# Joining token-major weight units to 512 columns and queueing weight splits behind the activations' low parts

## The chip, the cores and the metric

The kernel runs on one core of one Trainium2 chip. The metric is the device time of one execution in microseconds (us). Before the change it is 937.9 us, the median of three runs (937.23 to 940.86 us).

## The reference

The program is a chain of five residual stages on 256 tokens of width 1024, all in fp32:

```
h = swiglu(rms(x), ffn1_w_in, ffn1_w_out)          # 1024 -> 2 x 2816 -> 1024
x = x + 0.5 * rms(h)
x = x + rms(token_mixing(rms(x)))                  # retention + neighbourhood attention
h = swiglu(rms(x), ffn2_w_in, ffn2_w_out)
x = x + 0.5 * rms(h)
x = x + recurrent_mixer(rms(x))                    # y * silu(gate), width 1536
x = x + shortconv_mixer(rms(x))                    # bg * conv(cg * xv) * silu(gate), width 1536
return rms(x)
```

with `swiglu(x) = (silu(g) * u) @ w_out`, where g and u are the two halves of `x @ w_in`. Each stage begins with a normalised x and a product with a wide in-projection, and ends with an out-projection back to 1024 columns that is added to x. Nothing of the next stage's first product can start before x of a token is complete and its mean square is known.

## The kernel before

**Precision.** Every fp32 product is made of three faster ones. An operand is split into a high part (a rounded copy) and a low part (what the rounding left); `mm3` (L231 to L233) multiplies high by high, then the two mixed products. For weights the copy is L88 on ACT and the subtraction L90 on DVE, each over a part of 128 x 1024 numbers. For activations they are called ph and pl; those of the normed tile are L370 (ACT) and L371 (DVE).

**Weights.** All weights are listed in the order of use, in units of 256 columns cut into parts of 512 KB. `Stream` loads raw parts (L75, SP's queue), splits them (L88, L90) and hands them out from a ring of 41 slots. At most four raw parts wait unsplit, and up to 15 parts (AHEAD) are split ahead of the one in use; `use(p, most)` splits up to `most` parts on top of what p needs.

**Token tiles.** The 256 tokens are two tiles of 128, t = 0 and t = 1. `phase_b` is the out-projection. Its last parts are multiplied first for t = 0 and then for t = 1, so that `add_block` (L351, L354, L357) and the norm (`norm_of_x`, `inv_rms`) of t = 0 run beside the matmuls of t = 1. Four entries before the end, `ready(0)` has TensorE transpose the normed tile hn of t = 0 (L366, eight times 128 x 128), and ph and pl are taken out of PSUM. `phase_a` is the next in-projection. Its first `late` units are computed token-major: the activation is the stationary operand, 128 tokens by 256 weight columns, first for t = 0 and, after `ready(1)`, for t = 1. The result is then turned by transposes (`turn_tok`). All later units have the weights stationary and all 256 tokens of two column blocks as one 512-wide result. In the mixing stage the units computed first (queries and keys) are token-major anyway, with 512 columns.

**Order.** The tile framework's scheduler places every engine's instructions by its own model of time. `S.hold` names two instructions; splits that are issued later are kept behind them on ACT and on DVE. In the kernel before only the norm of x sets it. The bias loads of the attention (L118) and the mask additions on them (L624) are also placed by the scheduler, at the beginning of the mixing stage.

Of the kernel before, what the change touches and what calls it, by code (L numbers as in the profile page):

```python
# [29 lines left out]
class Part:  # L30


    def __init__(self, ap, whole):
        self.ap, self.whole = ap, whole
        self.a, self.n = ap.shape[1], ap.shape[1] * ap.shape[2]
        self.raw = self.hi = self.lo = None
# [5 lines left out]
class Unit:  # L42
    def __init__(self, ap, whole=False, most=1024):
        self.a = ap.shape[1]
        h = max(1, self.a * ap.shape[2] // most)
        h = self.a // h
        self.parts = [Part(ap[:, k:k + h, :], whole) for k in range(0, self.a, h)]


class Stream:  # L50
# [19 lines left out]
    def load(self, most=100):  # L70
        while (most and self.nd < len(self.parts) and self.nd - self.ns < self.ahead
# [3 lines left out]
            self.loaded = self.nc.sync.dma_start(out=p.raw, in_=p.ap)  # L75
# [50 lines left out]
def block_kernel(ctx: ExitStack, tc: tile.TileContext, A, C, out):  # L126
# [26 lines left out]

    def b_units(w):
# [31 lines left out]
    u_f2 = ffn_units(A["ffn2_w_in"], A["ffn2_w_out"])  # L186
# [173 lines left out]
    def transpose_pair(src, t, pair, k0, n):  # L360

        for b in range(0, n, 4):
# [7 lines left out]
            act.activation(out=h, in_=pv, func=AF.Copy)  # L370
            dve.tensor_tensor(out=lo, in0=pv, in1=h.bitcast(F32), op=ALU.subtract)  # L371
# [809 lines left out]
```

## Time and profile before

| | before |
|---|---|
| median of three runs | 937.9 us |
| profiled execution | 936.56 us |
| span, first to last instruction | 934.8 us |
| mean granted clock of TensorE | 0.997 of full speed |
| PE, DVE, ACT busy | 98%, 60%, 50% of the span |
| DMA, mean | 180 GB/s |

Mixing, the second feed-forward stage, recurrent and shortconv begin, by the transposes of their normed tile of t = 0, at 199, 438, 630 and 749 us. The profiled execution is 1.34 us shorter than the median of the runs, and 1.76 us of it lie outside the span. TensorE's matmuls overlap in the records (a 256-column one is shown as 0.28 us long but the next begins 0.12 us later), so their pace is read from start to start, not from their durations.

### The profile page before, as it was taken

What the parts mean: (1) busy time and instruction counts of PE and PEld (TensorE: products, weight loads), DVE (VectorE), ACT (ScalarE), POOL (GpSimd) and SP (SyncE); (2) the same over time, 40 slices, a digit from 0 to 9 for tenths busy, and PEclk for the clock granted to TensorE, in tenths of its full rate; (3) what the DMA queues carried; (4) which work ended last, traced back from release to release, by engine and by line L of the source; (5) the groups of instructions that cost most, each with busy time, mean ns of one, the idle gap of its engine ahead of it and who ended that gap; (6) DMA issues with size and microseconds to landing.
All of it is one profiled execution on the core that took longest, in us unless ns stands there. A gap on an engine that the chain in (4) does not pass through costs nothing.

```text
span 934.8 us, 15539 instructions
## 1 busy us (share of the span) xinstructions
PE 914.8 (98%) x6378; PEld 853.9 (91%) x6378; DVE 561.7 (60%) x736; ACT 471.9 (50%) x666; POOL 13.1 (1%) x24
## 2 busy tenths in 40 slices
PE   8999999999999999999999999999999989999997
PEld 7999998877978899997999998888998889999986
DVE  7854647377745454667574445545787965756513
ACT  7744546245565444545554444434769845544401
POOL 0000000000000000000000000000000000000000
PEclk9999999999999999999999999999999999999999
DMA  9955557758436453676455556757426745645501
GB/s 317 339 182 158 175 169 248 258 108 253 150 106 217 133 161 114 225 236 208 142 181 165 165 158 211 242 165 246 137 91 211 235 151 183 221 165 186 160 1 46
DMA packets 132333, 168.70 MB, mean 180 GB/s; under 512 B 12065, under 2 KB 112165, under 8 KB 132262
## 3 DMA queue, kind: packets, MB, share of 16 engines
q1 hardware_dynamic: 131828, 167.11, 56.1%
q8 instruction: 50, 0.82, 0.4%
q10 hardware_dynamic: 434, 0.59, 0.2%
q14 instruction: 21, 0.17, 0.1%
HBM read 166.64 MB, written 1.05 MB: 179 GB/s over the span
## 4 chain that ended last, share of the span: by engine, by line
PE 86%; DVE 5%; ACT 4%; issue 2%; SPq 1%; DMA 1%; POOL 0%; POOLq 0%; DVEq 0%; ACTq 0%
PE bank L233 27%; PE bank L231 27%; PE bank L232 27%; DVE lo L90 2%; SPq L118 1%; DVE ri L1030 1%; PE bank L743 1%; PE bank L768 1%; DMA t<-in_na_rel_bias 1%; ACT hi L88 1%; PE bank L366 1%; ACT ri L971 1%; ACT u L970 0%; PE bank L456 0%; PE bank L653 0%
## 5 line engine op out<-in xcount | busy, mean ns | idle before, releaser
L90 DVE TENSOR_TENSOR lo<-raw,hi 128x1024 fp32r<-128x1024 f32 (+1 forms) x302 | 359.1, 1216 | 130.3 <-ACT hi L88 75.1
L231 PE MATMUL bank<-ph,hi 128*128 128x256 f32 x1360 | 387.0, 285 | 0.0
L232 PE MATMUL bank<-pl,hi 128*128 128x256 f32 x1360 | 384.9, 283 | 0.0
L233 PE MATMUL bank<-ph,lo 128*128 128x256 f32 x1360 | 384.8, 283 | 0.0
L88 ACT ACTIVATE hi<-raw 128x1024 fp32r<-128x1024 f32 (+1 forms) x302 | 306.3, 1048 | 148.5 <-PE bank L233 70.3
L232 PEld LDWEIGHTS bank<-pl,hi 128*128 128x128 f32 x1360 | 261.0, 192 | 0.2
L231 PEld LDWEIGHTS bank<-ph,hi 128*128 128x128 f32 x1360 | 261.0, 192 | 0.2
L233 PEld LDWEIGHTS bank<-ph,lo 128*128 128x128 f32 x1360 | 261.0, 192 | 0.0
L231 PE MATMUL bank<-hi,ph 128*128 128x512 f32 (+1 forms) x636 | 225.6, 356 | 4.2 <-ACT ph L370 4.1
L233 PE MATMUL bank<-hi,pl 128*128 128x512 f32 (+1 forms) x636 | 222.4, 354 | 5.4 <-DVE pl L371 5.4
L232 PE MATMUL bank<-lo,ph 128*128 128x512 f32 (+1 forms) x636 | 223.3, 353 | 0.0
L231 PEld LDWEIGHTS bank<-hi,ph 128*128 128x128 f32 x636 | 121.2, 191 | 23.6 <-ACT ph L370 6.8
L233 PEld LDWEIGHTS bank<-hi,pl 128*128 128x128 f32 x636 | 120.3, 190 | 22.8 <-DVE pl L371 6.9
L232 PEld LDWEIGHTS bank<-lo,ph 128*128 128x128 f32 x636 | 121.2, 191 | 15.6
L470 ACT ACTIVATE ph<-tmp 128x512 fp32r<-128x512 f32 x28 | 17.6, 629 | 58.4 <-DVE tmp L492 53.8
L321 ACT ACTIVATE tmp<-x 128x512 f32<-128x512 f32 (+1 forms) x25 | 15.4, 614 | 50.1 <-DVE x L346 34.0
L492 DVE TENSOR_TENSOR tmp<-tmp,bank 128x512 f32<-128x512 f32 x19 | 13.0, 686 | 33.8 <-PE bank L233 33.8
L471 DVE TENSOR_TENSOR pl<-tmp,ph 128x512 fp32r<-128x512 f32 x28 | 19.2, 691 | 13.0 <-ACT ph L470 13.0
L354 DVE TENSOR_TENSOR tmp<-bank,g 128x512 f32<-128x512 f32 x12 | 8.3, 689 | 29.9 <-ACT tmp L351 29.9
L351 ACT ACTIVATE tmp<-bank 128x512 f32<-128x512 f32 x12 | 7.2, 600 | 36.3 <-PE bank L233 36.1
L371 DVE TENSOR_TENSOR pl<-bank,ph 128x512 fp32r<-128x512 f32 x24 | 15.7, 686 | 12.9 <-ACT ph L370 12.9
L313 POOL TENSOR_TENSOR small<-small,half 128x1 f32<-128x1 f32 x18 | 10.8, 601 | 811.1 <-DVE small L311 811.1
(141 smaller groups left out, 434.1 us busy)
## 6 DMA issues: line engine op xcount, KB each, us to landing
raw<-in_ffn_w_in SPq DMA_DIRECT2D x86, 512.0 KB, 4.6
raw<-in_w_mix_in SPq DMA_DIRECT2D x52, 512.0 KB, 4.5
raw<-in_b_w_in SPq DMA_DIRECT2D x48, 512.0 KB, 4.5
raw<-in_ffn_w_out SPq DMA_DIRECT2D x44, 512.0 KB, 4.1
raw<-in_a_w_in SPq DMA_DIRECT2D x24, 512.0 KB, 4.0
raw<-in_a_w_out SPq DMA_DIRECT2D x12, 512.0 KB, 3.6
raw<-in_b_w_out SPq DMA_DIRECT2D x12, 512.0 KB, 3.9
raw<-in_w_ret_out SPq DMA_DIRECT2D x8, 512.0 KB, 4.5
```

The costliest lines, as they stand in the source:

```text
L88: self.copied = self.nc.scalar.activation(out=p.hi, in_=p.raw, func=AF.Copy)
L90: self.nc.vector.tensor_tensor(out=p.lo, in0=p.raw, in1=p.hi.bitcast(F32), op=ALU.subtract)
L118: self.nc.sync.dma_start(out=out, in_=ap)
L231: pe.matmul(ps, a[0], b[0], start=first, stop=False)
L232: pe.matmul(ps, a[0], b[1], start=False, stop=False)
L233: pe.matmul(ps, a[1], b[0], start=False, stop=last)
L313: nc.gpsimd.tensor_tensor(out=r, in0=v, in1=half[:, 0:1], op=ALU.pow)
L321: sq = act.activation(out=tmp()[:, :c1 - c0], in_=x[:, t, c0:c1], func=AF.Square, scale=1.0 / 32, accum_out=ss[:, c:c + 1])
L371: dve.tensor_tensor(out=lo, in0=pv, in1=h.bitcast(F32), op=ALU.subtract)
L470: act.activation(out=h, in_=src, func=AF.Copy)
L471: dve.tensor_tensor(out=lo, in0=src, in1=h.bitcast(F32), op=ALU.subtract)
L492: dve.tensor_tensor(out=sg, in0=sg, in1=b, op=ALU.mult)
```

## The change

1. Two 256-column units that are used token-major become one unit of 512 columns (`pair_unit`): gate and up columns in the two feed-forward stages (one such pair in the first, in parts of half the size, two in the second), two gate units in the recurrent stage (one 256-column unit stays beside them), and the four column groups of the first block in shortconv, as two pairs. A part of a pair is two row blocks by 2 x 256 columns and is loaded by two DMAs of 256 KB. The products that follow the matmul (`tok_evac`) are now made in token-major form, before the turn; shortconv so turns two results where it turned four.
2. `ready(0)` is called six entries before the end of `phase_b` instead of four, and until then the t = 1 entries ask for no split ahead. In `phase_a` the t = 0 pass asks for none either before `ready(1)`, which comes `lead` parts before the end of that pass (0 in the first feed-forward stage, 2 in the second, 1 in recurrent, 2 in shortconv; in mixing 2 parts before).
3. `ready()` sets `S.hold` to its own two last evictions, so that weight splits issued later stand behind ph on ACT and pl on DVE.

```
             p.raw = p.view(self.slot(F32, "raw"))
-            self.loaded = self.nc.sync.dma_start(out=p.raw, in_=p.ap)
+            if len(p.ap.shape) == 3:
+                self.loaded = self.nc.sync.dma_start(out=p.raw, in_=p.ap)
+            else:
+                to = p.raw.rearrange("p a (z c) -> p a z c", z=p.ap.shape[2])
+                for z in range(p.ap.shape[2]):
+                    self.loaded = self.nc.sync.dma_start(out=to[:, :, z, :], in_=p.ap[:, :, z, :])
             self.nd += 1
             most -= 1
...
+    def pair_unit(w, c0, c1, most=1024):
+
+        v = w[:, c0:c0 + 256].rearrange("(k p) c -> p k c", p=128)
+        l = [list(d) for d in v.ap]
+        return Unit(bass.AP(tensor=v.tensor, offset=v.offset, ap=[l[0], l[1], [c1 - c0, 2], l[2]]), most=most)
+
...
-    def ffn_units(win, wout, small=False):
-        g, u = a_units(win, 0, DFF), a_units(win, DFF, 2 * DFF)
-        if small:
-            g[0] = Unit(win[:, 0:256].rearrange("(k p) c -> p k c", p=128), most=512)
-        return add([x for p in zip(g, u) for x in p]), add(b_units(wout))
-
-    u_f1 = ffn_units(A["ffn1_w_in"], A["ffn1_w_out"], True)
+    def ffn_units(win, wout, tok, most=1024):
+        first = [pair_unit(win, c, DFF + c, most) for c in range(0, 256 * tok, 256)]
+        g, u = a_units(win, 256 * tok, DFF), a_units(win, DFF + 256 * tok, 2 * DFF)
+        return add(first), add([x for p in zip(g, u) for x in p]), add(b_units(wout))
+
...
-    u_ag = a_units(A["a_w_in_2"], 0, WIDTH)
-    add(u_ag[:EARLY] + [ax[0], ax[1], u_gw[0], ax[2], u_gw[1], ax[3], ax[4], u_gw[2], ax[5]] + u_ag[EARLY:])
+    u_ag = a_units(A["a_w_in_2"], 256 * EARLY, WIDTH)
+    u_at = [pair_unit(A["a_w_in_2"], 0, 256)] + a_units(A["a_w_in_2"], 512, 256 * EARLY)
+    add(u_at + [ax[0], ax[1], u_gw[0], ax[2], u_gw[1], ax[3], ax[4], u_gw[2], ax[5]] + u_ag)
...
-    u_b = [[Unit(bw[:, s * WIDTH + c:s * WIDTH + c + 256].rearrange("(k p) c -> p k c", p=128))
-            for s in (1, 2, 0, 3)] for c in range(0, WIDTH, 256)]
-    for us in u_b:
-        add(us)
+    u_bt = add([pair_unit(bw, WIDTH, 2 * WIDTH), pair_unit(bw, 0, 3 * WIDTH)])
+    u_b = add([Unit(bw[:, s * WIDTH + c:s * WIDTH + c + 256].rearrange("(k p) c -> p k c", p=128))
+               for c in range(256, WIDTH, 256) for s in (1, 2, 0, 3)])
...
-    def mm_tok(bk, u, xt, t):
-
-        for q, p in enumerate(u.parts):
-            if t == 0:
-                S.use(p, 1)
-            for j in range(p.a):
-                k = q * p.a + j
-                mm3(bk[:, t * 256:(t + 1) * 256], xt.at(k, t * 128, t * 128 + 128),
-                    (p.hi[:, j, :], p.lo[:, j, :]), k == 0, k == u.a - 1)
-            if t == 1:
-                S.done(p)
+    def mm_tok(ps, u, q, xt, t):
+
+        p = u.parts[q]
+        for j in range(p.a):
+            k = q * p.a + j
+            mm3(ps, xt.at(k, t * 128, t * 128 + 128), (p.hi[:, j, :], p.lo[:, j, :]), k == 0, k == u.a - 1)
 
     def mm_t(ps, p, xt, t, k0, nk):
...
-            act.activation(out=h, in_=pv, func=AF.Copy)
-            dve.tensor_tensor(out=lo, in0=pv, in1=h.bitcast(F32), op=ALU.subtract)
+            a = act.activation(out=h, in_=pv, func=AF.Copy)
+            d = dve.tensor_tensor(out=lo, in0=pv, in1=h.bitcast(F32), op=ALU.subtract)
+        return a.ins, d.ins
...
-            transpose_pair(self.hn[t], t, self.pair, 0, NKD)
+            S.hold = transpose_pair(self.hn[t], t, self.pair, 0, NKD)
...
-            if q == len(order) - 4 and not last:
+            if q == len(order) - 6 and not last:
                 nxt.ready(0)
                 S.reserve = 0
             if a[0] is acc[t][0]:
-                S.use(p, 1)
+                S.use(p, 1 if t == 0 or last or nxt.pair else 0)
             mm_b(a, p, xt, t, k, n)
             if a[-1] is acc[t][-1]:
...
-    def phase_a(us, nxt, evac, late, tok_evac=None):
+    def phase_a(tok, us, nxt, evac, tok_evac, lead):
+
 
 
         xt = nxt.pair
         banks = []
-        for u in us[:late]:
-            b = bank()
-            banks.append(b)
-            mm_tok(b, u, xt, 0)
-        nxt.ready(1)
-        turned = None
-        for i, u in enumerate(us):
-            if i < late:
-                b = banks[i]
-                mm_tok(b, u, xt, 1)
+        for u in tok:
+            if u.w == 512:
+                banks.append([bank(), bank()])
             else:
                 b = bank()
-                mm_a2(b, u, xt)
+                banks.append([b[:, 0:256], b[:, 256:512]])
+        n = sum(len(u.parts) for u in tok)
+        for u, b in zip(tok, banks):
+            for q, p in enumerate(u.parts):
+                if n == lead:
+                    nxt.ready(1)
+                S.use(p, 0 if n > lead else 1)
+                mm_tok(b[0], u, q, xt, 0)
+                n -= 1
+        if lead == 0:
+            nxt.ready(1)
+        turned = None
+        for i, (u, b) in enumerate(zip(tok, banks)):
+            for q, p in enumerate(u.parts):
+                S.use(p, 1)
+                mm_tok(b[1], u, q, xt, 1)
+                S.done(p)
+            if turned:
+                turned()
+            turned = tok_evac(i, b)
+        for i, u in enumerate(us):
+            b = bank()
+            mm_a2(b, u, xt)
             if turned:
                 turned()
                 turned = None
-            if i < late:
-                turned = (tok_evac or turn_evac(evac))(i, b)
-            else:
-                evac(i, b)
+            evac(i, b)
         return xt
...
         for t in range(2):
-            if t == 1:
-                nxt.ready(1)
             for z in range(2):
                 ps = [p for u in qk_units[z] for p in u.parts]
                 for i, p in enumerate(ps):
-                    if t == 0:
-                        S.use(p)
+                    if (t, z, i) == (0, 1, 2):
+                        nxt.ready(1)
+                    S.use(p, 1 if (t, z, i) >= (0, 1, 2) else 0)
                     mm_t(acc[z][t], p, xt, t, 2 * i, NKD)
                     if t == 1:
                         S.done(p)
...
         def tok_evac(i, b):
-            if i % 2 == 0:
-                held[i] = b
-                return None
-            g = held.pop(i - 1)
             sg = tmp()
-            act.activation(out=sg, in_=g, func=AF.Silu)
-            dve.tensor_tensor(out=sg, in0=sg, in1=b, op=ALU.mult)
-            return lambda: split_pair(f, i - 1, 2, two(turn_tok(sg)))
-
-        xt = phase_a(us[0], nxt, evac, late, tok_evac)
+            for t in range(2):
+                s = sg[:, t * 256:(t + 1) * 256]
+                act.activation(out=s, in_=b[t][:, 0:256], func=AF.Silu)
+                dve.tensor_tensor(out=s, in0=s, in1=b[t][:, 256:512], op=ALU.mult)
+            return lambda: split_pair(f, 2 * i, 2, two(turn_tok(sg)))
+
```

In all, 576 MATMULs of 256 columns go and 288 of 512 columns come; transposes of results go from 64 to 56; SP issues 376 DMAs instead of 346. Lines move: L90 is now L96, L366 is L372, L370 is L376, L371 is L377, L354 is L360, L357 is L363, L624 is L635.

DVE's queue at the boundary from mixing to the second feed-forward stage, from the norm of t = 0 on (hn is the normed tile, L311 a scalar of the norm, small its result). Before:

```order
L90 TENSOR_TENSOR lo<-raw,hi 128x1024 x3
L354 TENSOR_TENSOR tmp<-bank,g 128x512
L90 TENSOR_TENSOR lo<-raw,hi 128x1024 x2
L354 TENSOR_TENSOR tmp<-bank,g 128x512
L311 TENSOR_SCALAR small<-small 128x1
L371 TENSOR_TENSOR pl<-bank,ph 128x4x128 x2
L357 SCALAR_TENSOR_TENSOR x<-tmp,small,x 128x512 x2
L327 TENSOR_TENSOR hn<-x,g 128x512 x2
```

The same place in the changed kernel:

```order
L360 TENSOR_TENSOR tmp<-bank,g 128x512
L377 TENSOR_TENSOR pl<-bank,ph 128x4x128
L360 TENSOR_TENSOR tmp<-bank,g 128x512
L317 TENSOR_SCALAR small<-small 128x1
L377 TENSOR_TENSOR pl<-bank,ph 128x4x128
L363 SCALAR_TENSOR_TENSOR x<-tmp,small,x 128x512 x2
L96 TENSOR_TENSOR lo<-raw,hi 128x1024
L333 TENSOR_TENSOR hn<-x,g 128x512
```

The five weight splits that stood ahead of the first pl are gone from there, and single ones now stand among the steps of x and hn of t = 1.

DVE's queue at the beginning of mixing, from the norm of t = 1 to its pl (t_2194 and the like are bias tiles, rot lines the rotary step). Before:

```order
L624 TENSOR_TENSOR t_2194<-t_2194,mask 128x768
L339 TENSOR_SCALAR hn<-hn,small 128x512 x2
L624 TENSOR_TENSOR t_2195<-t_2195,mask 128x768
L588 TENSOR_TENSOR tmp<-bank,rot 128x512
L590 SCALAR_TENSOR_TENSOR tmp<-bank,rot 128x4x64
L592 TENSOR_TENSOR tmp<-bank,rot 128x4x64
L624 TENSOR_TENSOR t_2196<-t_2196,mask 128x768
L593 TENSOR_TENSOR tmp<-tmp 128x512
L371 TENSOR_TENSOR pl<-bank,ph 128x4x128 x2
```

The same place in the changed kernel:

```order
L345 TENSOR_SCALAR hn<-hn,small 128x512 x2
L599 TENSOR_TENSOR tmp<-bank,rot 128x512
L601 SCALAR_TENSOR_TENSOR tmp<-bank,rot 128x4x64
L603 TENSOR_TENSOR tmp<-bank,rot 128x4x64
L604 TENSOR_TENSOR tmp<-tmp 128x512
L635 TENSOR_TENSOR t_2154<-t_2154,mask 128x768
L377 TENSOR_TENSOR pl<-bank,ph 128x4x128
L635 TENSOR_TENSOR t_2155<-t_2155,mask 128x768
L377 TENSOR_TENSOR pl<-bank,ph 128x4x128
```

The norm of t = 1 no longer stands behind a mask addition, and one addition instead of three stands ahead of the first pl.

DVE's queue at the boundary from recurrent to shortconv, up to the norm of t = 1. Before:

```order
L90 TENSOR_TENSOR lo<-raw,hi 128x1024
L327 TENSOR_TENSOR hn<-x,g 128x512
L90 TENSOR_TENSOR lo<-raw,hi 128x1024
L346 TENSOR_TENSOR x<-bank,x 128x512
L371 TENSOR_TENSOR pl<-bank,ph 128x4x128 x2
L327 TENSOR_TENSOR hn<-x,g 128x512
L311 TENSOR_SCALAR small<-small 128x1
L339 TENSOR_SCALAR hn<-hn,small 128x512 x2
```

The same place in the changed kernel:

```order
L333 TENSOR_TENSOR hn<-x,g 128x512
L352 TENSOR_TENSOR x<-bank,x 128x512
L333 TENSOR_TENSOR hn<-x,g 128x512
L377 TENSOR_TENSOR pl<-bank,ph 128x4x128
L317 TENSOR_SCALAR small<-small 128x1
L377 TENSOR_TENSOR pl<-bank,ph 128x4x128
L345 TENSOR_SCALAR hn<-hn,small 128x512 x2
L96 TENSOR_TENSOR lo<-raw,hi 128x1024 x2
```

The splits between the steps of x and hn have moved behind the norm, and both steps of hn now stand ahead of pl.

## Rows read from the trace of the kernel before

**Rows 1.** PE's waits: engine, line, who was waited for: us, times, longest.

```profile
PE bank L233 <- DVE pl L371: 5.4, 5, 1.6
PE bank L231 <- ACT ph L370: 4.1, 7, 1.4
```

**Rows 2.** Timeline of PE, steady stretches: start, us, engine, line, what, idle before.

```profile
23.39 0.28 PE L232 MATMUL bank<-pl,hi 128*128 128x256 f32 x1
...
28.91 0.28 PE L233 MATMUL bank<-ph,lo 128*128 128x256 f32 x1
...
424.08 0.39 PE L232 MATMUL bank<-lo,ph 128*128 128x512 f32 x1
...
426.80 0.39 PE L233 MATMUL bank<-hi,pl 128*128 128x512 f32 x1
```

**Rows 3.** Timeline of PE, mixing to the second feed-forward stage.

```profile
438.14 1.04 PE L366 MATMUL bank<-ident,hn 128*128 128x128 f32 x8
439.57 0.38 PE L231 MATMUL bank<-hi,ph 128*128 128x256 f32 x1 [0.39 <-ACT ph L370]
...
442.41 0.39 PE L233 MATMUL bank<-hi,pl 128*128 128x256 f32 x1 [1.63 <-DVE pl L371]
442.64 0.28 PE L231 MATMUL bank<-hi,ph 128*128 128x256 f32 x1
...
453.07 1.04 PE L366 MATMUL bank<-ident,hn 128*128 128x128 f32 x8
454.36 0.38 PE L231 MATMUL bank<-hi,ph 128*128 128x256 f32 x1 [0.25 <-ACT ph L370]
```

**Rows 4.** Timeline of DVE, the same boundary.

```profile
438.68 2.35 DVE L90 TENSOR_TENSOR lo<-raw,hi 128x1024 fp32r<-128x1024 f32 x2
440.95 0.69 DVE L354 TENSOR_TENSOR tmp<-bank,g 128x512 f32<-128x512 f32 x1
...
441.67 1.28 DVE L371 TENSOR_TENSOR pl<-bank,ph 128x512 fp32r<-128x512 f32 x2
```

**Rows 5.** Timeline of PE, first feed-forward stage to mixing.

```profile
199.02 1.04 PE L366 MATMUL bank<-ident,hn 128*128 128x128 f32 x8
...
202.04 0.50 PE L233 MATMUL bank<-hi,pl 128*128 128x512 f32 x1 [0.54 <-DVE pl L371]
...
216.24 0.65 PE L233 MATMUL bank<-hi,pl 128*128 128x512 f32 x1 [1.37 <-DVE pl L371]
```

**Rows 6.** Stretch of PE's writes to banks: stretch, us, busy (count), clock, DMA share, GB/s.

```profile
216.40:219.80 3.40, 3.40 (x9) 0.50 0.75 205
```

**Rows 7.** Timelines of DVE and of SP's queue at the beginning of mixing.

```profile
214.03 0.96 DVE L624 TENSOR_TENSOR t<-t,mask 128x768 f32<-128x768 f32 x1 [1.06 <-DMA t<-in_na_rel_bias]
...
215.50 1.28 DVE L371 TENSOR_TENSOR pl<-bank,ph 128x512 fp32r<-128x512 f32 x2
...
198.24 14.22 SPq L118 DMA_DIRECT2D t<-in_na_rel_bias  x16
```

**Rows 8.** Timeline of PE, into recurrent (630) and into shortconv (749).

```profile
630.16 1.03 PE L366 MATMUL bank<-ident,hn 128*128 128x128 f32 x8
...
633.97 0.39 PE L233 MATMUL bank<-hi,pl 128*128 128x256 f32 x1 [0.30 <-DVE pl L371]
...
749.36 1.03 PE L366 MATMUL bank<-ident,hn 128*128 128x128 f32 x8
...
754.59 0.39 PE L233 MATMUL bank<-hi,pl 128*128 128x256 f32 x1 [1.56 <-DVE pl L371]
```

**Rows 9.** Costliest groups: line, what, count | busy, mean ns | idle before, releaser.

```profile
L88 ACT ACTIVATE hi<-raw 128x1024 fp32r<-128x1024 f32 (+1 forms) x302 | 306.3, 1048 | 148.5 <-PE bank L233 70.3
```

**Rows 10.** DMA issues: what, queue, count, KB each, us from issue to landing.

```profile
raw<-in_ffn_w_in SPq DMA_DIRECT2D x86, 512.0 KB, 4.6
raw<-in_ffn_w_in SPq DMA_DIRECT2D x4, 256.0 KB, 4.8
```

**Rows 11.** Stretch into shortconv: us, busy of PE, PEld, DVE, ACT, POOL, clock, DMA share, GB/s.

```profile
750.00:755.00 5.00, 2.01 (x15) 1.57 (x14) 5.00 (x7) 2.72 (x7) 0.00 (x0) 1.00 1.02 340
```

More of the change, by code (lines that the diff above doesn't have):

```diff
@@ L44, in __init__ @@
         self.a = ap.shape[1]
-        h = max(1, self.a * ap.shape[2] // most)
+        self.w = int(np.prod(ap.shape[2:]))
+        h = max(1, self.a * self.w // most)
         h = self.a // h
-        self.parts = [Part(ap[:, k:k + h, :], whole) for k in range(0, self.a, h)]
+        self.parts = [Part(ap[:, k:k + h], whole) for k in range(0, self.a, h)]
 class Stream:
@@ L458, in turn_tok @@
         return ps
-    def turn_evac(evac):
-        def first(i, b):
-            s = tmp()
-            act.activation(out=s, in_=b, func=AF.Copy)
-            return lambda: evac(i, turn_tok(s))
-        return first
     def split_pair(pair, k, n, src):
@@ L478, in two, with ffn @@
         return ap.rearrange("p (k t) -> p k t", k=2)
-    def ffn(us, nxt, post, next_ap, late, aside=None):
+    def ffn(us, nxt, post, next_ap, lead, aside=None):
         f = Pair(NKF)
         held = {}
+        done = 2 * len(us[0])
         def evac(i, b):
@@ L994, in recurrent, with tok_evac, evac @@
         early = []
[L996 to L1009 removed]
+        def tok_evac(i, b):
+            gs = []
+            for c in range(0, u_at[i].w, 256):
+                g = tmp()
+                for t in range(2):
+                    act.activation(out=g[:, t * 256:(t + 1) * 256], in_=b[t][:, c:c + 256], func=AF.Silu)
+                gs.append(g)
+            def turned():
+                for z, g in enumerate(gs):
+                    j = 2 * i + z
+                    if j % 2 == 0:
+                        early.append(S.slot(F32, "early"))
+                    act.activation(out=early[j // 2][:, (j % 2) * 512:(j % 2 + 1) * 512], in_=turn_tok(g),
+                                   func=AF.Copy)
+            return turned
+        def evac(j, b):
             conv(j, b)
@@ L1040, in recurrent @@
         banks = []
-        xt = phase_a(u_ag[:EARLY] + u_ax, nxt, evac, LATE_R, tok_evac)
-        for j, u in enumerate(u_ag[EARLY:]):
+        xt = phase_a(u_at, u_ax, nxt, evac, tok_evac, 1)
+        for j, u in enumerate(u_ag):
             b = bank()
@@ L1083, in evac, with tok_evac, turned @@
                                              op0=ALU.mult, op1=ALU.add)
+            for g in got:
+                dve.tensor_tensor(out=o, in0=o, in1=g, op=ALU.mult)
+            split_pair(y, 2 * j, 2, two(o))
+        def evac(i, b):
+            held.append(b)
+            if i % 4 != 3:
+                return
+            cg, xv, bg, gt = held
+            held.clear()
+            w = tmp()
+            act.activation(out=w, in_=cg, func=AF.Copy)
+            dve.tensor_tensor(out=w, in0=w, in1=xv, op=ALU.mult)
             sg = tmp()
             act.activation(out=sg, in_=gt, func=AF.Silu)
-            dve.tensor_tensor(out=o, in0=o, in1=bg, op=ALU.mult)
-            dve.tensor_tensor(out=o, in0=o, in1=sg, op=ALU.mult)
-            split_pair(y, 2 * j, 2, two(o))
-        xt = phase_a([u for us in u_b for u in us], nxt, evac, LATE_A)
+            convolved(1 + i // 4, w, (bg, sg))
+        def tok_evac(i, b):
+            w = tmp()
+            for t in range(2):
+                s, p0, p1 = w[:, t * 256:(t + 1) * 256], b[t][:, 0:256], b[t][:, 256:512]
+                if i == 0:
+                    act.activation(out=s, in_=p0, func=AF.Copy)
+                    dve.tensor_tensor(out=s, in0=s, in1=p1, op=ALU.mult)
+                else:
+                    act.activation(out=s, in_=p1, func=AF.Silu)
+                    dve.tensor_tensor(out=s, in0=s, in1=p0, op=ALU.mult)
+            def turned():
+                held.append(turn_tok(w))
+                if i == 1:
+                    a, g = held
+                    held.clear()
+                    convolved(0, a, (g,))
+            return turned
+        xt = phase_a(u_bt, u_b, nxt, evac, tok_evac, 2)
         xt.drop()
         return phase_b(u_bo, y, None, False, A["final_g_2"], LATE_B, last=True)
-    LATE_1, LATE_A, LATE_B, LATE_R, LATE_O = 2, 4, 4, 3, 3
+    LATE_B, LATE_O = 4, 3
     def prepare():
```

37 lines of the change are left out of this document (10 added, 27 removed).

## Prediction

> **What bounds the kernel now.** I read the busy shares first (the table above): TensorE is busy for 98% of the span, so the time is the number of matmuls times their pace, plus the places where TensorE stands still. The view of waits came next, and it names these places: 5.4 us in five waits for pl on DVE and 4.1 us in seven for ph on ACT [rows 1]. Then the timelines around these waits. They lie where a stage begins, four times in the program, and the reader is to see the same figure in each: eight transposes, a few products that need only ph, a stop until DVE has made pl [rows 3, 5, 8]. DVE isn't idle in that stop; it subtracts weights [rows 4]. Everywhere else the engines beside TensorE have spare time, and what they gain or lose there doesn't reach the end.
>
> **Pace.** From 23.39 to 28.91 us stand 46 starts of 256-column matmuls, 0.120 us each; from 424.08 to 426.80 stand 12 of 512 columns, 0.227 us each [rows 2]. Joining two to one saves 2 x 0.120 - 0.227 = 0.0133 us. 288 joins make 3.8 us: 0.64 for each pair unit (8 row blocks, 3 products, 2 tiles = 48 joins), of which there are one, two, one and two in the four stages concerned. Eight transposes fewer are, by the rows of eight that take 1.04 us with the last one's tail, about 0.109 us each, 0.9 us. These 4.7 us are sure so long as TensorE is the bound.
>
> The Trainium skill, "TensorE: Matmul & The Clock Gate", section "Back-to-back issue gap", gives the isolated spacing of a warm matmul as N / 2.4 plus 2.5 ns, so that a join would save only those 2.5 ns. By that rule the 288 joins would give 0.7 us. The trace disagrees: its 256-column spacing is 120 ns and not 109, and I take the trace.
>
> **What the stops cost now.** Idle time is less than what is lost, since a stopped array also drains and starts slowly. Mixing to the second feed-forward stage [rows 3]: from the first transpose at 438.14 to the second matmul after the stop at 442.64 are 4.50 us. At pace, eight transposes (0.87) and nine matmuls (1.08) take 1.95. Lost: 2.55 us, where the rows list 0.39 + 1.63 = 2.02 idle, so each of the two stops costs 0.27 more than its idle time. With tile t = 1 (453.07 to 454.36) 1.29 - 0.87 + 0.10 for the slow start = 0.5 us go.
> - First feed-forward stage to mixing [rows 5]: 199.02 to 202.04 are 3.02 us for 0.87 + 5 x 0.227; with the slow start 1.1 us lost. For t = 1 TensorE stops 1.37 us before 216.24, 1.6 lost; right behind, nine matmuls run at half the clock, 1.2 instead of 2.4 GHz, in 3.40 us [rows 6] where 9 x 0.227 = 2.04 would do, 1.4 lost. Together 4.1.
> - Into recurrent [rows 8]: 630.16 to 633.97 are 3.81 us for 0.87 + 0.227 + 6 x 0.120, with the slow start 2.1; t = 1 as above, 0.5.
> - Into shortconv [rows 8]: 749.36 to 754.59 are 5.23 us for 0.87 + 8 x 0.120, with the slow start 3.5; t = 1 again 0.5.
>
> Sum: 4.1 + 3.05 + 2.6 + 4.0 = 13.8 us. The other way round, 9.5 us of idle [rows 1] plus 12 stops at 0.27 plus 1.4 of slow clock make 14.1.
>
> **What the hold does to them.** At 438.68 DVE begins two weight splits, 2.35 us, then 0.69 for L354 and only at 441.67 pl [rows 4]. In the changed order no split stands there: pl of the first four blocks comes right behind its ph. With the splits gone, pl's first half is there some 0.7 us after ph, while TensorE has several 512-column products of 0.227 us that need ph alone; its second half has the first half's twelve products (2.7 us) to hide in, and needs 0.69 + 0.21 + 0.69 of them. What is late next is ph itself: the 0.39 us of idle at 439.57 [rows 3], with drain and slow start 0.66. The earlier call of the transposes doesn't help much there: in TensorE's order they still stand one matmul ahead of the end of the out-projection, since hn is not ready sooner. So I leave 0.5 to 0.66 at each of the four boundaries, 2.3 in all. The stop for t = 1 goes where `lead` parts of t = 0 stand behind the transposes (two parts are 12 products, 2.7 us, over the 1.3 that ph and the transposes took), and that is so into the second feed-forward stage, recurrent and shortconv.
>
> Into shortconv three splits leave the stretch before pl, which gives the same picture: at 1.18 us each (2.35 for two) they are 3.5 us, just the loss counted there.
>
> In mixing pl of t = 1 stands behind three mask additions that wait for bias loads (1.06 us of idle before the one at 214.03, 0.96 us of work), whose sixteen issues take SP's queue from 198.24 on for 14.22 us [rows 7]. In the changed order one addition is left ahead of pl, and the transposes come two parts sooner. Bounds: if that one still waits as the one at 214.03 did, 1.06 + 0.96 stay and half of the 3.0 us of t = 1 is saved; if its load is there, all of it, the half clock too. I take 2.8, since the norm of t = 1 no longer waits behind such an addition either.
>
> **What is added, and its cover.** `use` without splits ahead lets the stock of split parts fall, by up to five at a boundary; it is counted at nothing, since up to 15 are kept and since almost half of ACT's idle time before its copies (70.3 of 148.5 us) was waiting for slots that TensorE had to free [rows 9]: splitting is ahead most of the time. Without that cover each late part costs a DVE split, 1.18 us. The 256-column evictions are more instructions on ACT and DVE beside TensorE's 512-column stream: nothing, or, if one is waited for, some tenths of a us (0.69 is a whole 512-wide one). The pairs' 40 DMAs of 256 KB for 20 of 512 KB land after 4.8 against 4.6 us [rows 10], with four raw parts ahead: nothing, or the price of the last rival. The start gains its joins only. The small stops inside recurrent I leave as they are.
>
> **Sum.** 3.8 + 0.9 + (13.8 - 2.3) = 16.2 us. The profiled execution took 936.56; it becomes 920.4. The median of the runs stands 1.34 above it, so I predict 921.7 us. If no stop is left and the mixing stage gains all, 918; about that much on the other side, with waits of 0.5 us more at each of eight places, is 925.
>
> **The rivals.**
> - *Half of the stops come back elsewhere.* The order after puts single splits between x and hn of t = 1, and a norm behind pl; each delays the second normed tile, and TensorE may wait for hn where it waited for pl. Half of 13.8 saved: 936.56 - 4.7 - 6.9 + 1.34 = 926.3. For it: ph and hn are now next in the chain. Against it: t = 1 of mixing's successor came 10 us after DVE's pl [rows 3, 4], and `lead` uses at most 2.7 of them.
> - *The stops stay.* The order is made by a model of time, so ph may be late for reasons that it doesn't know. Only joins and turns pay: 936.56 - 4.7 + 1.34 = 933.2. Against it: pl stood behind work that visibly is gone from there.
> - *The stock runs dry, slower.* Five parts are held back at three boundaries and three at the last: 18 parts x 1.18 = 21 us if TensorE must wait for each of them, 943. It takes back the gain from 14 parts on, and is slower by more than 0.5% only when all are exposed. Rows 9 speak against it.
> - *Half-size loads hold up the queue, slower.* If a DMA costs its queue the same whatever its size, then, at the 340 GB/s reached at 750 us [rows 11], 512 KB per 1.54 us, 20 more make 31 us; exposed entirely that is 953, and it decides from 21 us on. For it: a 256 KB load took no less time to land than one of 512 KB [rows 10]. Against: loads that wait side by side share that time, and the stretches with pairs lie behind ones in which SP waits for slots.
>
> The Trainium skill, "DMA: Bandwidth & Descriptors", section "Anatomy of one DMA", puts about 2.0 us of fixed cost on each DMA beside bytes / 436e9, from a fit for another queue's path; that would make this rival 20 x 2.0 = 40 us by estimate, if nothing of it overlapped. The landing times of rows 10 agree that size is not what sets them; whether the fixed part overlaps no row shows.
>
> **Chances.** Forecast 0.67 (its own range 918 to 925), half back 0.17, stops stay 0.10, stock dry 0.03, loads 0.03. The range 918 to 930 takes in the first two; about 0.18 is left out. Some 0.5% (4.7 us) is what a measurement can tell from no change. Faster by more: the first two and a little under half of the third, 0.87; within: the rest of the third and mild forms of the last two, 0.09; slower 0.04.
>
> **What would show it.** In the profile after: waits for pl below 1.5 us in total and none over 0.6; waits for ph still some 2 to 3 us; no stretch at half clock near 216; 512-column matmuls at 0.227 at each stage's beginning; no wait of TensorE for a weight's hi or lo, and none for a DMA beyond the start. Wrong would be: a new wait for hn before the second set of transposes (first rival), unchanged waits for pl (second), waits for lo or hi of weights just after a boundary (third), or ACT's copies waiting for raw loads in the second feed-forward stage and shortconv (fourth).

## The result and the profile after

The changed kernel takes 922.71 us (median of four runs, 922.03 to 924.21), 0.9841 times the time before (95% interval 0.9809 to 0.9874; the kernel before took 937.57 in the same comparison). Predicted were 921.7. Its profiled execution took 922.03 us with a span of 920.2, so 14.6 us of span went where 16.2 were forecast.

The view of waits answers to [rows 1]; the columns are the same, and here stands the whole answer for TensorE:

```profile
PE bank L1144 <- DMA g<-in_ffn_pre_norm: 2.3, 1, 2.3
PE bank L372 <- DMA raw<-in_ffn_w_in: 1.5, 1, 1.5
PE bank L242 <- ACT ph L376: 1.1, 4, 0.3
PE bank L945 <- DVE u L975: 0.9, 1, 0.9
```

Each line gives the sum in us, the number of waits and the longest. The wait for pl, 5.4 us before, is gone from the list; ph is left with 1.1 us in four waits. The timeline of TensorE shows where they are. The first transposes of the four later stages, and around them the places of [rows 3, 5, 8]:

```profile
199.26 1.04 PE L372 MATMUL bank<-ident,hn 128*128 128x128 f32 x8
...
434.08 1.04 PE L372 MATMUL bank<-ident,hn 128*128 128x128 f32 x8
434.87 0.48 PE L244 MATMUL bank<-hi,pl 128*128 128x512 f32 x1
435.37 0.50 PE L242 MATMUL bank<-hi,ph 128*128 128x512 f32 x1
435.70 0.39 PE L243 MATMUL bank<-lo,ph 128*128 128x512 f32 x1
...
446.39 1.04 PE L372 MATMUL bank<-ident,hn 128*128 128x128 f32 x8
447.68 0.50 PE L242 MATMUL bank<-hi,ph 128*128 128x512 f32 x1 [0.25 <-ACT ph L376]
...
622.91 1.04 PE L372 MATMUL bank<-ident,hn 128*128 128x128 f32 x8
...
739.97 1.03 PE L372 MATMUL bank<-ident,hn 128*128 128x128 f32 x8
741.31 0.50 PE L242 MATMUL bank<-hi,ph 128*128 128x512 f32 x1 [0.31 <-ACT ph L376]
...
742.63 0.50 PE L244 MATMUL bank<-hi,pl 128*128 128x512 f32 x1
```

Into the second feed-forward stage the transposes at 434.08 are followed by products almost at once; before, 2.55 us were lost there. From 434.08 to 435.70 are 1.62 us, and eight transposes and two products at pace take 0.87 + 0.45: 0.3 us are lost. The second stop of that stage (behind the transposes at 446.39) still has its 0.25 us of idle, as at 454.36 before. DVE's timeline at the same place answers to [rows 4]:

```profile
435.35 0.69 DVE L377 TENSOR_TENSOR pl<-bank,ph 128x512 fp32r<-128x512 f32 x1 [2.10 <-ACT ph L376]
436.11 0.69 DVE L360 TENSOR_TENSOR tmp<-bank,g 128x512 f32<-128x512 f32 x1
436.72 0.20 DVE L317 TENSOR_SCALAR small<-small 128x1 f32<-128x1 f32 x1
436.84 0.68 DVE L377 TENSOR_TENSOR pl<-bank,ph 128x512 fp32r<-128x512 f32 x1
```

Now DVE has been idle for 2.10 us when ph comes, and pl is made at once. At the beginning of mixing the half clock of [rows 6] is gone. The stretch from 212 to 224 us (columns as in [rows 11]) shows the clock at full speed, and SP's queue issues the bias loads from 194.00 on, 4.2 us sooner than in [rows 7]:

```profile
212.00:224.00 12.00, 11.75 (x56) 9.62 (x55) 9.22 (x11) 6.89 (x8) 0.00 (x0) 1.00 0.89 234
```

```profile
194.00 15.67 SPq L124 DMA_DIRECT2D t<-in_na_rel_bias  x16
```

From the first transposes of one stage to those of the next (start and end of the span at the outside), in us, with the 16.2 of the prediction divided in the same way:

| | to mixing | mixing | second feed-forward | recurrent | shortconv |
|---|---|---|---|---|---|
| before | 199.0 | 239.1 | 192.0 | 119.2 | 185.4 |
| after | 199.3 | 234.8 | 188.8 | 117.1 | 180.2 |
| measured | +0.2 | -4.3 | -3.2 | -2.1 | -5.2 |
| forecast | -0.6 | -3.5 | -3.8 | -2.7 | -5.6 |

### The profile page after: what moved, and what is told of

It is laid out like the page before. It is cut to its first block, busy times and chain, and to the rows that moved or that the text cites. A ratio compares the mean times of both kernels' runs of the same rounds, so it can differ in the third digit from the quotient of the medians.

```text
span 920.2 us, 15017 instructions
## 1 busy us (share of the span) xinstructions
PE 908.0 (99%) x6082; PEld 836.0 (91%) x6082; DVE 564.4 (61%) x743; ACT 471.3 (51%) x672; POOL 13.1 (1%) x24
## 4 chain that ended last, share of the span: by engine, by line
PE 90%; ACT 4%; DVE 3%; DMA 1%; issue 1%; SPq 0%; POOL 0%; POOLq 0%; DVEq 0%; ACTq 0%
PE bank L242 29%; PE bank L243 28%; PE bank L244 28%; PE bank L372 1%; DVE lo L96 1%; DVE ri L1045 1%; PE bank L754 1%; PE bank L779 1%; ACT hi L94 1%; DMA raw<-in_b_w_in 1%; ACT ri L982 1%; ACT u L981 1%; PE bank L664 0%; ACT ri L960 0%; DMA x<-in_x 0%
## 5 line engine op out<-in xcount | busy, mean ns | idle before, releaser
L96 DVE TENSOR_TENSOR lo<-raw,hi 128x1024 fp32r<-128x1024 f32 (+1 forms) x304 | 360.1, 1209 | 137.1 <-ACT hi L94 75.2
L242 PE MATMUL bank<-hi,ph 128*128 128x512 f32 (+1 forms) x540 | 208.8, 387 | 1.1 <-ACT ph L376 1.1
L243 PE MATMUL bank<-lo,ph 128*128 128x512 f32 (+1 forms) x540 | 206.5, 383 | 0.0
L244 PE MATMUL bank<-hi,pl 128*128 128x512 f32 (+1 forms) x540 | 205.2, 383 | 0.1
L242 PEld LDWEIGHTS bank<-hi,ph 128*128 128x128 f32 x540 | 101.9, 189 | 23.5 <-ACT ph L376 3.2
L244 PEld LDWEIGHTS bank<-hi,pl 128*128 128x128 f32 x540 | 101.7, 189 | 20.4 <-DVE pl L377 0.8
L243 PEld LDWEIGHTS bank<-lo,ph 128*128 128x128 f32 x540 | 102.0, 189 | 19.6 <-DVE lo L96 0.6
L360 DVE TENSOR_TENSOR tmp<-bank,g 128x512 f32<-128x512 f32 x12 | 8.3, 692 | 36.0 <-ACT tmp L357 35.7
L357 ACT ACTIVATE tmp<-bank 128x512 f32<-128x512 f32 x12 | 7.2, 599 | 42.7 <-PE bank L244 42.4
L377 DVE TENSOR_TENSOR pl<-bank,ph 128x512 fp32r<-128x512 f32 x24 | 16.0, 686 | 14.2 <-ACT ph L376 14.2
```

What stands on the lines that cost most here:

```text
L96: self.nc.vector.tensor_tensor(out=p.lo, in0=p.raw, in1=p.hi.bitcast(F32), op=ALU.subtract)
L242: pe.matmul(ps, a[0], b[0], start=first, stop=False)
L243: pe.matmul(ps, a[0], b[1], start=False, stop=False)
L244: pe.matmul(ps, a[1], b[0], start=False, stop=last)
L377: d = dve.tensor_tensor(out=lo, in0=pv, in1=h.bitcast(F32), op=ALU.subtract)
```

## The experiments

The theory at first was the prediction's: joins and turns pay 4.7 us by TensorE's pace, and the hold on ph and pl keeps weight splits from before pl, which pays 11.5. The rivals: asking for no splits ahead is what clears DVE's queue; the earlier calls are; the joins alone are. Each run below the first row was compared with the kernel before on the same chip in five rounds; three chips were used, so runs are compared with each other by their ratios first. The stage columns (ffn 2 is the second feed-forward stage) are those of one execution, the profiled one, as in the table above; the last column is the sum over the stages, the span.

| run | ratio to before (95%) | median | to mixing | mixing | ffn 2 | recurrent | shortconv | span |
|---|---|---|---|---|---|---|---|---|
| changed kernel | 0.9841 (0.9809 to 0.9874) | 922.71 | 199.3 | 234.8 | 188.8 | 117.1 | 180.2 | 920.2 |
| joins alone | 0.9969 (0.9956 to 0.9983) | 935.7 | 199.9 | 239.7 | 189.7 | 119.7 | 184.7 | 933.7 |
| hold alone | 1.0003 (0.9987 to 1.0019) | 938.22 | 199.0 | 239.5 | 192.0 | 119.2 | 185.4 | 935.0 |
| none asked alone | 0.9910 (0.9889 to 0.9930) | 929.4 | 199.1 | 235.7 | 190.6 | 119.5 | 182.8 | 927.7 |
| no hold | 0.9850 (0.9830 to 0.9871) | 924.49 | 201.0 | 234.8 | 189.9 | 117.7 | 180.3 | 923.7 |
| splits asked | 0.9936 (0.9913 to 0.9959) | 932.41 | 199.5 | 239.2 | 189.6 | 116.9 | 185.5 | 930.6 |
| asked in pass | 0.9854 (0.9830 to 0.9877) | 924.48 | 199.9 | 234.8 | 189.9 | 117.7 | 180.3 | 922.6 |
| calls late | 0.9858 (0.9832 to 0.9884) | 923.81 | 199.6 | 235.5 | 188.3 | 117.9 | 180.7 | 922.0 |
| halves | 0.9877 (0.9857 to 0.9896) | 926.51 | 200.3 | 234.8 | 189.7 | 117.6 | 181.8 | 924.3 |
| x sooner | 0.9831 (0.9806 to 0.9856) | 922.14 | 199.0 | 234.8 | 188.8 | 117.1 | 180.4 | 920.1 |
| none in t = 1 | 0.9841 (0.9814 to 0.9868) | 923.05 | 199.9 | 235.5 | 189.1 | 116.9 | 180.4 | 921.8 |
| lead four | 0.9836 (0.9809 to 0.9863) | 922.74 | 198.7 | 235.5 | 189.1 | 116.9 | 180.3 | 920.5 |
| four loads | 0.9882 (0.9859 to 0.9904) | 926.51 | 200.7 | 235.0 | 189.0 | 119.6 | 180.2 | 924.6 |

**Joins alone.** The new units and products; `ready` and `use` as before, no hold.

```
-                S.use(p, 1 if t == 0 or last or nxt.pair else 0)
+                S.use(p, 1)
...
-            S.hold = transpose_pair(self.hn[t], t, self.pair, 0, NKD)
+            transpose_pair(self.hn[t], t, self.pair, 0, NKD)
```

(and in the same way the calls and asks of `phase_a` and mixing.)

> The joined units and their token-major products alone; the calls of ready, the splits asked for ahead and the hold are as before. If the joins pay by TensorE's pace (288 x 0.0133 us + 0.9 us of turns, less the 0.9 us that the start lost in the changed kernel), the median is 933 to 934.5 and the waits for pl stay at 4 to 5 us. If joining also removes the stops at stage beginnings (rival), it is below 928 and waits for pl are under 2 us.

Measured: 2.9 us less (0.0031 of 938), 935.7 where 933 to 934.5 were expected. TensorE's waits for pl are as long in sum as before:

```profile
PE bank L244 <- DVE pl L377: 5.3, 5, 2.3
PE bank L242 <- ACT ph L376: 4.5, 6, 1.4
```

The joins don't take the stops away; they shift them. Into the second feed-forward stage the stop for pl shrinks from 1.63 us to 0.62, at mixing's second transposes it grows from 1.37 to 2.25. By the stages the joins gain 2.3 us in the second feed-forward stage but only 0.7 in shortconv, and the first stage is 0.9 longer; why shortconv is so short of 0.64 x 2 + 0.9 is seen in the run with splits asked. Part of what is missing is clock: the twelve executions have a mean granted clock of 0.992 to 0.997, and the three at 0.997 took 932.7 to 934.2 us, against 936.5 to 938.9 for the kernel before at 0.997 on that chip, a difference of 3.5 us by the medians.

**Hold alone.** The kernel before with part 3 of the change only.

```
-            transpose_pair(self.hn[t], t, self.pair, 0, NKD)
+            S.hold = transpose_pair(self.hn[t], t, self.pair, 0, NKD)
```

> The kernel before with the hold on ph and pl alone. If the hold keeps splits from before pl: 926 to 929, waits for pl under 2 us. If it doesn't, since the splits that stand there were asked for before ready is called (what the two runs without hold and with splits asked point to): 937 to 939, no difference from before, waits for pl 5 to 5.5 us.

Measured: no difference, and the waits are those of before:

```profile
PE bank L233 <- DVE pl L371: 5.9, 5, 1.9
PE bank L231 <- ACT ph L370: 4.1, 7, 1.4
```

The step to which the prediction gave 11.5 us gives nothing by itself.

**No hold.** The changed kernel without part 3.

```
-            S.hold = transpose_pair(self.hn[t], t, self.pair, 0, NKD)
+            transpose_pair(self.hn[t], t, self.pair, 0, NKD)
```

> The changed kernel without the hold on ph and pl. If the hold is what keeps splits behind pl, as the prediction credits it, the waits for pl come back: 930 to 933. If the splits are out of the way because none is asked for ahead in those passes (rival), the time stays at 922 to 923 and the waits for pl stay under 1.5 us.

Measured: 0.985, within the interval of the changed kernel; mixing and shortconv are as short as with it. The second feed-forward stage and recurrent are 1.1 and 0.7 longer by their stops for t = 1, where a wait of 1.32 us for ph (before the product at 450.45) and one of 0.40 for pl (638.85) stand. A wait of 1.32 for a weight's hi lies elsewhere, at 13.20 in the first stage. By the medians the hold is worth at most 1.8 us, by the ratios 0.8 (0.0009 of 938), which the intervals can't tell from nothing.

**Splits asked.** The changed kernel with hold and early calls, but asking ahead as before.

```
-                S.use(p, 1 if t == 0 or last or nxt.pair else 0)
+                S.use(p, 1)
...
-                S.use(p, 0 if n > lead else 1)
+                S.use(p, 1)
...
-                    S.use(p, 1 if (t, z, i) >= (0, 1, 2) else 0)
+                    if t == 0:
+                        S.use(p)
```

> The changed kernel with the hold, but every pass asks for splits ahead as before (1 per part, 2 in mixing). If the hold does it: 922 to 923.5, waits for pl under 1.5 us. If asking for none does it (rival): splits stand before pl again at the four boundaries, 9 to 11 us come back, 931 to 933, waits for pl 4 to 5 us, and the stretch at half clock at the beginning of mixing with them.

Measured: 0.9936, 8.9 us (0.0095 of 938) given back. TensorE's waits, and DVE at the place of [rows 4]:

```profile
PE bank L244 <- DVE pl L377: 4.4, 4, 1.7
```

```profile
438.71 2.35 DVE L96 TENSOR_TENSOR lo<-raw,hi 128x1024 fp32r<-128x1024 f32 x2
440.97 0.68 DVE L377 TENSOR_TENSOR pl<-bank,ph 128x512 fp32r<-128x512 f32 x1
```

The two splits are back ahead of pl, hold or no hold. So is the slow stretch of mixing: from 212 to 224 us the clock is 0.86 on the mean, as products at half pace (0.426 us from start to start) follow a stop of 1.72 us for pl:

```profile
212.00:224.00 12.00, 10.04 (x42) 7.91 (x41) 6.06 (x10) 3.33 (x5) 0.00 (x0) 0.86 0.75 181
```

Shortconv, 5.3 longer, has the same two stops as the kernel before, of which the second stands in [rows 8] and the first is

```profile
751.82 0.39 PE L231 MATMUL bank<-hi,ph 128*128 128x256 f32 x1 [1.43 <-ACT ph L370]
```

but in this execution a stretch at half clock follows them, which there was none of in the profiled execution of the kernel before:

```profile
747.57 0.50 PE L242 MATMUL bank<-hi,ph 128*128 128x512 f32 x1 [1.43 <-ACT ph L376]
...
750.34 0.80 PE L244 MATMUL bank<-hi,pl 128*128 128x512 f32 x1 [1.57 <-DVE pl L377]
750.93 0.63 PE L242 MATMUL bank<-hi,ph 128*128 128x512 f32 x1
...
756.05 0.44 PE L242 MATMUL bank<-hi,ph 128*128 128x512 f32 x1
```

Twelve starts take 5.12 us there where 12 x 0.227 = 2.7 would do: 2.4 us of the 5.3. In the run with joins alone the same stretch is 754.87 to 757.31 us, six products, and costs 1.1 us.

The hold can only move splits that are issued after `ready`; those in the way were asked for earlier, while t = 1 of the out-projection ran.

**None asked alone.** The kernel before, only without asks ahead in these passes.

```
-                S.use(p, 1)
+                S.use(p, 1 if t == 0 or last or nxt.pair else 0)
...
-                    if t == 0:
-                        S.use(p)
+                    S.use(p, t)
```

(The second edit is mixing's; `mm_tok` has the same. The asks left out of the t = 0 pass are so made in the t = 1 pass, as in the changed kernel.)

> The kernel before, 256-column units, calls and hold as they were, but no split asked for ahead in the t = 1 entries of phase_b before ready(0), nor in the t = 0 pass of phase_a and of mixing. If this is the part that takes the stops away: 9 us under before, 928 to 930, waits for pl under 1.5 us, no half clock in mixing. If it works only together with the earlier calls or with the hold: 934 to 938.

Measured: 8.4 us less (0.009 of 938), 929.4 as expected, without joins, hold or calls. Waits for pl fall to 1.1 us, and from 212 to 224 us the clock is 1.00:

```profile
PE bank L231 <- ACT ph L369: 1.7, 6, 0.4
PE bank L233 <- DVE pl L370: 1.1, 2, 0.9
```

This one part does most of the work: 8.4 of 14.9 us (0.0159 of 938). The joins alone give 2.9. The remaining 3.6 were not run by themselves; undone singly, the earlier calls take back 1.6 by the ratios and the hold 0.8.

**Asked in pass.** Asks back in the t = 0 passes of `phase_a` and mixing only; still none at the end of `phase_b`.

> The changed kernel, but the t = 0 passes of phase_a and of mixing ask for splits ahead as before; the t = 1 entries of phase_b still ask for none before ready(0). The run with splits asked everywhere gave back 10.4 us of span: by its stops 0.8 + 0.9 + 5.2 at the first pl of three stages and 3.4 at mixing's second one, half clock included. If the end of phase_b is what counts for pl of t = 0, only mixing's 3.4 come back here, 925 to 927, and mixing's first stop and shortconv's stay at 0.4 and 1.0. If the passes of phase_a do most of it (rival), 929 or more and waits for pl over 3 us.

Measured: neither expectation held in full. Mixing stays at 234.8, so that its second stop and the half clock hang on the end of `phase_b` too. By the timeline, the asks at the end of `phase_b` are also what kept the bias loads back (they are issued from 198.7 on in the run with splits asked, from 194.6 here and 194.0 in the changed kernel). What comes back is 1.1 in the second feed-forward stage and 0.7 in recurrent, just as without the hold. Of the 10.4 us of span that asking everywhere costs, 8.0 (930.6 - 922.6) hang on the end of `phase_b`. The opposite, asks back at the end of `phase_b` alone, gave no time: with them the ring of 41 slots is full before the program is through. So this share is a difference of two runs.

**Calls late.** `ready(0)` at four entries as before, `ready(1)` after the whole pass.

```
-            if q == len(order) - 6 and not last:
+            if q == len(order) - 4 and not last:
...
-    xt = phase_a(u_bt, u_b, nxt, evac, tok_evac, 2)
+    xt = phase_a(u_bt, u_b, nxt, evac, tok_evac, 0)
```

(and in the same way in mixing, recurrent and the second feed-forward stage.)

> The changed kernel with ready(0) four entries before the end as before, and ready(1) after the whole pass of t = 0 in every stage; no splits ahead, hold and joins as changed. By the prediction the earlier call gives 0.2 us and 0.5 us where the second transposes have products behind them: 922.5 to 924. If the earlier calls are a condition of the gain (rival): above 926, with waits for pl or for hn over 3 us.

Measured: 923.81, within what was expected; 1.8 us of span more than the changed kernel, by mixing (0.7), recurrent (0.8), shortconv (0.5) and the start (0.3), with the second feed-forward stage 0.5 shorter. The earlier calls (part 2 of the change) are worth about what was forecast, and are no condition for the rest.

**Halves.** Each 512-column product of the token-major units done as two of 256 in the same bank.

```
-            mm3(ps, xt.at(...), (p.hi[:, j, :], p.lo[:, j, :]), ...)
+            for c in range(0, u.w, 256):
+                mm3(ps[:, c:c + 256], xt.at(...), (p.hi[:, j, c:c + 256], p.lo[:, j, c:c + 256]), ...)
```

> The changed kernel, loads and splits and evictions as they are, but each token-major matmul of 512 columns done as two of 256. If a join saves 13.3 ns, 288 times that come back: 926 to 927 (3.8 us above the changed kernel). If it saves 2.5 ns each, 0.7 us: not distinguishable from the changed kernel, 922.5 to 923.5. If the joins' gain is hidden behind waits for ph, also under 1 us.

Measured: 926.51. That is 3.4 us more by the ratios (0.9877 - 0.9841 of 938), 3.8 by the medians, 4.1 by the spans. The 13.3 ns of [rows 2] stand; the 2.5 ns that the prediction weighed against them would have given 0.7 us back, and no execution of this run (925.8 to 927.7) is as short as the changed kernel's longest (924.2).

**X sooner.** The load of x for t = 1 behind four small weight loads, not eight.

```
-    S.load(4)
+    S.load(2)
     nc.sync.dma_start(out=x[:, 1, :], in_=xin[:, 1, :])
```

> The changed kernel with the load of x for t = 1 issued behind four instead of eight of the small weight DMAs. If that issue (6.0 us after the start, 3.7 before the change) is what made the first stage no shorter, the second transposes come 1 us sooner and mixing's first transposes at 198 to 199 us: 921 to 922. If the start is bound by the splits of the joined parts (rival), mixing begins at 199.3 to 201 as in the changed kernel and the time is 922.5 to 923.5.

Measured: mixing begins at 199.0 instead of 199.3; the variants without this edit begin it between 199.5 and 201.0. The time isn't distinguishable from the changed kernel's. SP's queue, in the changed kernel and then here:

```profile
1.65 4.32 SPq L81 DMA_DIRECT2D raw<-in_ffn_w_in  x8
6.02 0.43 SPq L236 DMA_DIRECT2D x<-in_x  x1
```

```profile
1.65 1.85 SPq L81 DMA_DIRECT2D raw<-in_ffn_w_in  x4
3.54 0.43 SPq L236 DMA_DIRECT2D x<-in_x  x1
```

Even with the load 2.5 us sooner the stage isn't shorter than before, although 48 joins should give 0.64: TensorE waits here, with a joined pair, for splits of 512 columns (two waits for lo and one for hi, 0.8 us).

**None in t = 1** and **lead four.** Both with x sooner; no split ahead in any t = 1 entry, and in the second run also `ready(1)` four parts before the end of the pass in the second feed-forward stage. The edit for the splits:

```
-                S.use(p, 1 if t == 0 or last or nxt.pair else 0)
+                S.use(p, 1 if t == 0 or last else 0)
```

> The changed kernel with the load of x for t = 1 behind four small loads, and no split asked for ahead in any t = 1 entry of phase_b, so that none stands between x and hn of t = 1. If those two splits (2.4 us) are what makes the second normed tile late, the second transposes get products of t = 0 behind them in mixing and the second feed-forward stage, two stops of 0.5 us go, and with the start's 0.3 to 0.5 it is 921 to 922. If the stock of split parts gets too small by it (rival), TensorE waits for hi or lo of weights for over 1 us: 923 or more.

> As the run before (no split in t = 1, x sooner), with ready(1) four parts instead of two before the end of the t = 0 pass in the second feed-forward stage. If two parts were already enough to hide ph, the same time within 0.5 us, 921 to 922, and the wait for ph at that place absent in both; if hn of t = 1 is not there so soon (rival), a wait for hn of 1 us or more stands before those transposes, 922 to 923.5.

Measured: no gain in either (923.05 and 922.74; 921 to 922 were expected if the splits were the cause). Mixing is 0.7 longer than in the changed kernel; its second transposes now come at 208.3 to 209.5 instead of 211.6, but the stops around them grow from 0.5 to 1.2 us. With four parts of lead TensorE meets hn itself (a wait of 0.3 us). So nothing was gained by moving the splits from between x and hn of t = 1.

**Four loads.** Each large pair part by four DMAs of 128 KB.

> The changed kernel with each of the 20 large pair parts loaded by four DMAs of 128 KB instead of two of 256 KB, 40 DMAs more. If the loads run ahead and their number costs nothing, 922 to 923.5, no wait of TensorE for weights over 0.5 us. If a DMA costs its queue the same whatever its size (the prediction's last rival, 1.54 us each, 62 us for 40), part of it shows: 930 or more, and ACT's copies wait for raw loads at the beginning of the second feed-forward stage, recurrent and shortconv.

Measured: 3.8 us more than the changed kernel, where the rival asked for 930 or more. It isn't a price of each load: the second feed-forward stage and shortconv, which load eight pair parts each, are as long as in the changed kernel (189.0, 180.2). Recurrent carries 2.6, by one wait of 2.40 us for hn, ahead of which the order now has four splits on DVE:

```profile
744.37 1.11 PE L373 MATMUL bank<-ident,hn 128*128 128x128 f32 x8 [2.40 <-DVE hn L346]
```

The scheduler's order moved with the loads. The start has the other 1.4 us, and how much of that is scatter isn't settled.

## Why the prediction was right, and where its steps were not

- *Pace of joins and turns (4.7 us)*: right for the three later stages. Halving the products again costs 3.4 to 4.1 us, where 3.8 were forecast; the joins alone gave 2.9, with a first stage 0.9 longer and, in the profiled execution, 1.1 lost to half clock in shortconv.
- *The stops' cost (13.8 us) and what stays (2.3)*: the size is nearly right. In mixing the sum is 0.8 short:

```profile
213.44 0.50 PE L231 MATMUL bank<-hi,ph 128*128 128x512 f32 x1 [0.25 <-ACT ph L370]
...
219.99 0.39 PE L233 MATMUL bank<-hi,pl 128*128 128x512 f32 x1
```

  The first line, in the kernel before, is a stop of t = 1 for ph that was left out, 0.5 us lost in all; and the nine products at half clock begin at 216.24 and give way to the next at 219.99, 3.75 us and not the 3.40 of the window in [rows 6], so that 1.7 are lost and not 1.4. Of the stops 3.4 us stay. At the first pl of three stages 0.3 are left each, and 1.0 into shortconv, where a square still stands ahead of ph on ACT; at the second transposes 0.5 are left each into mixing, the second feed-forward stage and recurrent.
- *"What the hold does to them"*: the wrong cause. The hold alone gives nothing and taking it out costs at most 1.8 us; asking for no split ahead, which the prediction booked as an added cost "at nothing", gives 8.4 to 8.9. The sum came out right because the forecast rested on the order of instructions in the changed kernel, which has no splits there, and not on which edit took them away.
- *"The stop for t = 1 goes where `lead` parts stand behind the transposes"*: only into shortconv. In the changed order the second transposes stand right at the end of the t = 0 pass in the other stages, as at 446.39, and each costs its 0.25 us of idle, 0.5 us in all, as before. In the second feed-forward stage and recurrent together that is 1.0 us which the forecast didn't have.
- *"The start gains its joins only"*: it lost 0.2 instead of gaining 0.6. In the profiled execution TensorE's first transposes come at 7.62 us instead of 6.81, since ACT's square of the second half of x of t = 0 waits longer for its load (before, then after), and the norm behind it is as much later; in the list above this is TensorE's wait of 1.5 us at L372, put down there to a weight load:

```profile
4.37 0.63 ACT L321 ACTIVATE tmp<-x 128x512 f32<-128x512 f32 x1 [0.37 <-DMA x<-in_x]
```

```profile
5.18 0.63 ACT L327 ACTIVATE tmp<-x 128x512 f32<-128x512 f32 x1 [1.11 <-DMA x<-in_x]
```

  That isn't the whole of it: in the runs with no hold, splits asked and asked in pass, with the same order of loads, the transposes come at 6.8 and mixing begins no sooner. There TensorE waits for a weight's hi (0.5 to 1.3 us), as both halves of the joined columns must be split before the first products. Loading x for t = 1 sooner brought 0.3 us, within the scatter of these starts. How the 0.8 us divide stays open.
- *Luck in the sum.* By the stages the forecast gain was 0.8 us too high at the start, 0.6 each in the second feed-forward stage and recurrent and 0.4 in shortconv, and 0.8 too low in mixing. The last is about the 0.8 that the count of mixing's stops left out, and it covers the start's miss; that 1.6 us are left, and not 2.4, is luck.
- *The rivals.* Stops coming back elsewhere: only the 1.0 us of the second transposes. Stock of split parts dry: no wait for lo or hi in the changed kernel's list. Loads: twice as many cost the queue nothing visible, and in the changed kernel the issues of [rows 10] (same columns) read

```profile
raw<-in_ffn_w_in SPq DMA_DIRECT2D x76, 512.0 KB, 5.2
raw<-in_ffn_w_in SPq DMA_DIRECT2D x16, 256.0 KB, 5.4
raw<-in_ffn_w_in SPq DMA_DIRECT2D x16, 128.0 KB, 3.9
```

so that 512 and 256 KB land in about the same time, and 128 KB somewhat sooner.

No run beat the changed kernel by more than its interval; x sooner is lowest with 922.14.

## What to carry to other kernels

When a producer stands behind prefetch work on its engine, look for the place where that work is asked for: an ordering edge set at the producer can't move what was queued before it, but not asking in the last steps ahead of it can. Credit each part of a change by undoing it alone; an order of instructions that is right for the sum doesn't say which edit made it. Where a small stop is left, count what it costs beyond its idle time (0.25 us of idle cost 0.5 here) before moving the cause about, and expect that a scheduled order moves elsewhere with it.

## What the runs showed of the hardware

The granted clock fell to half not by the length of a stop alone. In the profiled execution of the kernel before, TensorE stopped for 0.39 and 1.63 us at 439 us [rows 3] and for 1.43 and 1.56 into shortconv [rows 8] and went on at full clock; at 216, after 1.37 us, it went on at half [rows 5, 6]. With joined products the same two stops into shortconv, 1.43 and 1.57 us, were followed by half clock in both runs that had them (joins alone, splits asked), for six and twelve starts in 2.4 and 5.1 us. The products around the stop were 512 columns wide in these three cases and 256 in the others, but width doesn't settle it: without the hold TensorE stopped for 1.32 us at 450 between joined products, and the clock stayed at 1.00 from 448 to 455.

Each of these is a single execution, and executions of one kernel differ. The 56 of the kernel before that ran beside the experiments have a mean granted clock from 0.991 to 0.999 and took from 942.4 down to 935.4 us, longer at the lower clock. A stretch like that of [rows 6] lowers the mean by 0.0018 (half of 3.4 us in 934.8), so that by this estimate some had none in mid-program and some several. Joins alone lay at 0.992 to 0.997, splits asked at 0.991 to 0.997, none asked alone at 0.998 to 0.999 (929.3 to 929.9 us) and the changed kernel at 0.996 to 0.999. So the kernels with long stops lose some us by the clock that change from one execution to the next, and taking the stops away takes most of that scatter away too. Whether joined products make it worse isn't shown.
